# A two-layer GLA and short-convolution step on one core: the sample's state products in column strips, the third token group's LayerNorm moved into the MLP, and the convolution's output projection in plain products

## The chip, the core and the metric

The kernel runs on one core of a Trainium2 chip. Its engines work side by side, each on its own list of instructions: TensorE (PE: matrix products; PEld are its weight loads), VectorE (DVE), ScalarE (ACT), GpSimd (POOL) and SyncE (SP), which here only issues transfers; POOL issues transfers too and sends most of the outputs. The metric is the device time of one execution in microseconds, the median of several runs. A profiled execution gives the trace.

## What is computed

One inference step over 1,056 tokens: a prompt of 1,024 and 8 sequences of 4 new tokens each (the samples). Layer 0 mixes by gated linear attention (GLA), layer 1 by a gated short convolution; a dense squared-ReLU MLP follows each. Cut to what matters:

```
D_MODEL, D_FF, GLA_HEADS = 1024, 4096, 4           # per head 128 q/k and 256 v channels
# GLA:  S_t = diag(exp(g_t)) S_{t-1} + k_t^T v_t ;  o_t = q_t S_t
#       each of the 8 sample sequences starts from a state s0 of its own (128 x 256 per head)
o = o * rsqrt(mean(o*o) + RMS_EPS) * norm_g;  f = (o * silu(r)) @ w_o
# convolution:
bg, cg, h = split(x @ w_in, 3);  u = cg * h
conv = sum_i full[:, i:i+t] * w_conv[i]            # full = the 2 rows of state, then u
f = (bg * conv) @ w_out                            # w_out is 1024 x 1024
# MLP:  f = square(relu(x @ w_up)) @ w_down
# after each of the four:  x = LayerNorm(ALPHA * x + f(x))
```

All is fp32. A product runs as three products of split operands: each operand is a high part (rounded to fp32r) and a low part (the rest), and high times high, high times low and low times high are added in PSUM.

## The kernel before, in words

Channels lie on partitions, tokens along the free axis. ScalarE makes a high part (`A.copy`) and VectorE the low part (`V.tensor_sub`): L847 and L848 in `split`, tiles `wh`/`wl` for weights and `bh`/`bl` for activations.

**GLA** works on three token groups, `TGS`, of 384, 384 and 288 tokens; the third holds the last 256 prompt tokens and the 32 sample tokens. Heads 0 to 3 come in turn. `ACC[tg]` (the tile `Z`) gathers the output projection over the heads. Projections are products of 384 or 288 columns from lines L236 to L238 (`mm3`), 24 of them for each unit of 128 output channels and each group. `mm` (L232) is a product in fp32 itself, and the trace shows each as two instructions. `sample(h)` treats the sample tokens of one head: its inner `outputs` makes 32 columns for each of two 128-channel halves `m`, from a product with the values `vt` plus, for each of the eight sequences, q (4 columns) times its own state `s0`. `outputs` is followed by `products` and `state`, which renew the state.

What runs beside what in this stage is a set of chains. `after(key, (delay, fn), ...)` puts one on, `tick()` runs the steps whose delay, in an estimated clock, has passed, and `need(key)` runs at once what is left of it. A scheduler then orders the instructions of PE, ACT and DVE; SP and POOL keep the written order. At the last head each group's output projection (`accumulate`, from `out(tg)`) ends in `layer_norm(tg, ...)`: the means are taken away, the squares added up, a product with ones (L309) gives the variance, `rstd` follows in ring tiles, and four `finish` steps multiply (L334, VectorE, two channel tiles each) and scale (L336, ScalarE, one channel tile each). All three chains end before the MLP begins.

**MLP and convolution** share a machine. A `Unit` is a weight tile of 128 x 512 (256 KB): loaded plainly (`raw`, on SP's queue) or as a sum of quarters (tile `SB`, the first part on SP's queue, the rest added by accumulating transfers on POOL's). `up` and `down` multiply in a scheme of seven products of matrix quarters in place of eight; sums of activations and outputs that the scheme needs are VectorE's. Tokens are cut in two halves of 528 (`TH`), and `product` (L865) does 3 matmuls for each of two tiles of 264 columns (`NT`). The work is a list of steps (`step`, `hook`), each with `prep` (split its weights and activations), `work_` (the matmuls) and `done`; `prep` runs two steps ahead. PSUM tiles there are four `ps2` of 1,024 columns.

L865 runs 13,440 matmuls: 5,376 in the first MLP, 2,016 in the convolution's input projections, 672 in its output projection (`down(..., True)`, seven products by four pairs) and 5,376 in the second MLP. After each `down` `norm(z, t, ...)` takes the LayerNorm of half `t` over five tiles of tokens: transposes by PE to tokens on partitions (L1175, eight a tile), statistics on VectorE, scaling on ScalarE (L1194), transposes back (L1202, eight a tile), and an eviction that applies gain and bias (L1206 on ScalarE, L1210 on VectorE). `states` writes out the convolution's new states.

Names of PSUM tiles are `ps` (GLA) and `pq` (later); `big` are norm's row tiles.

Of the kernel before, what the change touches and what calls it, by code (L numbers as in the profile page):

```python
# [9 lines left out]
F32 = mybir.dt.float32  # L10
# [3 lines left out]
ALU = mybir.AluOpType  # L14
# [43 lines left out]
def hybrid_step(ctx, tc, x_prompt, x_sample, state_gla, state_conv, gla_w_in, gla_w_gate_up, gla_b_gate,  # L58
# [91 lines left out]
    for g in (2, 3):  # L150
        V.tensor_add(seq, seq, seq1[:, g, :])


# [162 lines left out]
    def layer_norm(tg, sums, pg, pb):  # L316

        n = TGS[tg][1]
        z = ACC[tg]
        box = {}  # L320

        def split():
# [9 lines left out]
        def finish(k):  # L332
            pair = z[:, k:k + 2, :]
            V.tensor_tensor(pair, pair, box["rstd"][:, :n].unsqueeze(1).to_broadcast([P, 2, n]), op=ALU.mult)  # L334
# [126 lines left out]
    with tc.tile_pool(name="gp", bufs=3) as gp:  # L461
# [109 lines left out]

        def gated(tg, m, ur, o, tags=("g", "g")):
            n = TGS[tg][1]
# [7 lines left out]
            V.tensor_mul(sr[:, :n], o[:, m, :n], sr[:, :n])  # L581
            hh = gt(tags[0], [P, 384], 9 if tags[0] == "g" else 3, F32R)
            A.copy(hh[:, :n], sr[:, :n])
            hl = gt(tags[1], [P, 384], 9 if tags[1] == "g" else 3, F32R)
            V.tensor_sub(hl[:, :n], sr[:, :n], f32(hh[:, :n]))
            return hh[:, :n], hl[:, :n]

        def core(h, qkk, uv, dec, o):
# [77 lines left out]
            def sample(k2t, st, vt):  # L666
# [3 lines left out]
                box = []  # L670

                def outputs():
                    po = ps()
# [25 lines left out]

                after(("sample",), (0, outputs))  # L700

# [30 lines left out]
        for h in range(H):  # L732
# [34 lines left out]
            for tg in range(3):  # L767
                tags = [("g", "g")] * 2
                if last and tg == 2:
                    tags = [("b", "g"), ("b", "b")]  # L770
                hs.append([gated(tg, m, ur[m], o[tg], tags[m]) for m in range(2)])
                if tg == 2:
# [17 lines left out]
    explog()  # L790
    for tg in range(3):
        need(("x", tg))
# [19 lines left out]
    SB = work.tile([P, NB, 512], F32, name="SB")  # L812
    cbuf = work.tile([P, KC * 34], F32, name="cbuf")
    cst = cbuf[:, 0:KC * 16].rearrange("p (j s) -> p j s", s=16)
# [53 lines left out]
    class Unit:  # L868
# [33 lines left out]
        def split(self):  # L902
# [3 lines left out]
            return self.parts  # L906

    in_sb = {}
    ONE, TWO, SUM, ON1, ON2 = (11000,), (15000, 9000), (21000, 14000), (12000,), (17000, 9000)
# [5 lines left out]
    EARLY = ("sum", (21, 22), SUM)  # L915
    ALL = ("sum", (11, 12, 21, 22), (40000, 32000, 24000, 16000))

# [10 lines left out]
    def up(x, pairs, relu):  # L928
# [62 lines left out]
        for prod in UP:  # L991
            for i, (s, quad) in enumerate(pairs):
# [26 lines left out]
    def down(z, pairs, last, final=False):  # L1019
# [54 lines left out]
        def down_units(prod, g, *where):  # L1074
            if prod == 3 and n == 4:

                us = [Unit(pairs[i][1], ALL, i, *where) for i in g]
            else:
                us = [Unit(pairs[i][1], WDOWN[prod], pairs[i][0], *where) for i in g]
            return us, [Unit(pairs[i][1], EARLY, pairs[i][0]) for i in g if prod == 1]  # L1080
# [178 lines left out]
    def conv(x, z):  # L1259
# [40 lines left out]

        def quad_out(j):
            def q(ij):
                i, k = ij // 10 - 1, ij % 10 - 1
                r = (j + 4 * k) * P
                return conv_w_out[0, r:r + P, i * 512:i * 512 + 512]
            return q

        for g in range(2):
            js = (2 * g, 2 * g + 1)
# [53 lines left out]
    def rows_out(t):  # L1363
# [11 lines left out]
        if t < 6:  # L1375
            A.mul(yt[:tn, :], yt[:tn, :], r)  # L1376
        return (lambda: nc.gpsimd.dma_start(yt[:tn, :], end[1][:tn, :], accum_op=ALU.add),  # L1377
                lambda: nc.sync.dma_start(out, yt[:tn, :]))

    mlp(0, Z, Z2)  # L1380
    conv(Z2, Z)
# [54 lines left out]
```

## Time and profile before

| | |
|---|---|
| median of 3 runs | 2261.52 us (2258.97 to 2264.5) |
| the profiled execution | 2263.59 us, of which 2261.9 us are the span of the trace and 1.69 us lie around it |
| granted TensorE clock, mean | 0.983 |
| busy | PE 97%, DVE 72%, ACT 50%, POOL 23% |
| transfers | 251.51 MB, mean 111 GB/s |
| stages, by the trace | GLA's last product ends at 513 us; of L865 the first MLP's 5,376 matmuls begin at 531, the 2,016 of the convolution's input at 1202, the 672 of its output at 1455, the second MLP's at 1561; the last ends at 2244 |

The profiled execution is 2.07 us above the median. A count `xN` is a number of instructions. The idle time printed behind a group or in square brackets is that of the engine just before it, and what stands behind the arrow is what ended it. `PEclk` is the TensorE clock that was granted (1.00 is full speed). In rows of windows each engine's busy time is followed by its instructions, then come PEclk, the share of the DMA engines in use and GB/s.

### The profile page before, as it was taken

The numbers are of one execution on the slowest core, as the hardware profiler recorded it, in microseconds if no ns is written. First come the engines' busy times: TensorE is split into PE (matmuls) and PEld (weight loads), VectorE is DVE, ScalarE is ACT, GpSimd is POOL, SyncE is SP. The second block draws the span as 40 slices with busy tenths as digits, with TensorE's granted clock in tenths as the row PEclk, the third lists the DMA queues.
The fourth block names the chain that finished last, engine by engine and source line by source line (L and its number), as shares of the span: only waits on it lengthen the run. The fifth ranks groups of instructions, "written<-read, shape, count | busy, mean of one in ns | idle before, by whom it ended". The sixth has DMA issues, their size and how long they took to land. (4 is left out here: it accounts for less than half of the span.)

```text
span 2261.9 us, 43193 instructions
## 1 busy us (share of the span) xinstructions
PE 2202.5 (97%) x17341; PEld 2180.1 (96%) x17341; DVE 1619.5 (72%) x2982; ACT 1127.8 (50%) x2023; POOL 524.7 (23%) x551
## 2 busy tenths in 40 slices
PE   9999999996999999999999999998999999999996
PEld 8999999996999999999999999997999999999996
DVE  7474848467578864678787897996668875578877
ACT  4443525258563445564457444445855444654443
POOL 5202321221422021412021323220331101422121
PEclk9999999998999999999999999998999999999998
DMA  5120212113868456769353857760786734877546
GB/s 156 32 75 31 75 40 67 38 59 81 109 119 214 119 108 122 97 126 217 99 112 68 131 111 100 164 156 24 126 136 141 177 90 95 129 131 185 152 88 148
DMA packets 297476, 251.51 MB, mean 111 GB/s; under 512 B 15444, under 2 KB 238776, under 8 KB 297276
## 3 DMA queue, kind: packets, MB, share of 16 engines
q0 software_dynamic: 123200, 107.58, 31.2%
q1 hardware_dynamic: 174076, 141.18, 21.1%
q8 instruction: 136, 2.23, 0.4%
q14 instruction: 64, 0.52, 0.1%
HBM read 227.00 MB, written 9.12 MB: 104 GB/s over the span
## 5 line engine op out<-in xcount | busy, mean ns | idle before, releaser
L865 PE MATMUL pq<-bh,wh 128*128 128x264 f32 x4160 | 847.6, 285 | 9.3 <-ACT bh L847 7.3
L865 PE MATMUL pq<-bl,wh 128*128 128x264 f32 x4160 | 847.7, 285 | 5.0 <-DVE bl L848 5.0
L865 PE MATMUL pq<-bh,wl 128*128 128x264 f32 x4160 | 845.0, 285 | 1.8 <-DVE wl L848 1.7
L865 PEld LDWEIGHTS pq<-bh,wh 128*128 128x128 f32 x4160 | 646.2, 189 | 11.5 <-ACT bh L847 9.9
L865 PEld LDWEIGHTS pq<-bl,wh 128*128 128x128 f32 x4160 | 646.3, 189 | 6.1 <-DVE bl L848 5.8
L865 PEld LDWEIGHTS pq<-bh,wl 128*128 128x128 f32 x4160 | 646.2, 189 | 2.6 <-DVE wl L848 2.5
L847 ACT CAST wh<-raw 128x512 fp32r<-128x512 f32 x312 | 193.5, 621 | 398.2 <-PE pq L865 383.7
L848 DVE TENSOR_TENSOR wl<-raw,wh 128x512 fp32r<-128x512 f32 x312 | 214.4, 688 | 142.2 <-ACT wh L847 135.2
L854 POOL DMA_DIRECT2D SB<-in_mlp_w_up x128 | 163.5, 1329 | 430.8 <-DVE wl L848 223.8
L847 ACT CAST wh<-SB 128x512 fp32r<-128x512 f32 x208 | 128.7, 619 | 239.2 <-PE pq L865 213.4
L848 DVE TENSOR_TENSOR wl<-SB,wh 128x512 fp32r<-128x512 f32 x208 | 142.7, 686 | 85.3 <-ACT wh L847 85.3
L847 ACT CAST bh<-H 128x528 fp32r<-128x528 f32 (+1 forms) x292 | 165.3, 570 | 56.7 <-PE pq L865 51.3
L848 DVE TENSOR_TENSOR bl<-H,bh 128x528 fp32r<-128x528 f32 (+1 forms) x292 | 179.0, 625 | 15.4 <-ACT bh L847 15.2
L854 POOL DMA_DIRECT2D SB<-in_mlp_w_down x96 | 85.1, 1172 | 300.3 <-DVE wl L848 136.6
L236 PE MATMUL ps<-XH,whi 128*128 128x384 f32 (+1 forms) x384 | 128.6, 335 | 0.0
L237 PE MATMUL ps<-XL,whi 128*128 128x384 f32 (+1 forms) x384 | 127.5, 332 | 0.0
L238 PE MATMUL ps<-XH,wlo 128*128 128x384 f32 (+1 forms) x384 | 127.0, 331 | 0.0
L854 POOL DMA_DIRECT2D SB<-in_conv_w_in x48 | 61.2, 1295 | 168.8 <-DVE wl L848 60.4
L865 PE MATMUL pq<-bh,rh 128*128 128x264 f32 x320 | 94.0, 294 | 4.0 <-ACT bh L847 4.0
L865 PE MATMUL pq<-bl,rh 128*128 128x264 f32 x320 | 91.9, 287 | 0.2
L865 PE MATMUL pq<-bh,rl 128*128 128x264 f32 x320 | 91.5, 286 | 0.0
L963 ACT ACTIVATE H<-H 128x528 f32<-128x528 f32 x96 | 61.9, 645 | 46.9 <-DVE H L983 28.0
(275 smaller groups left out, 3620.4 us busy)
## 6 DMA issues: line engine op xcount, KB each, us to landing
raw<-in_mlp_w_down SPq DMA_DIRECT2D x160, 256.0 KB, 3.2
SB<-in_mlp_w_up POOLq DMA_DIRECT2D x128, 256.0 KB, 4.9
raw<-in_mlp_w_up SPq DMA_DIRECT2D x96, 256.0 KB, 2.9
SB<-in_mlp_w_down POOLq DMA_DIRECT2D x96, 256.0 KB, 7.8
SB<-in_mlp_w_up SPq DMA_DIRECT2D x64, 256.0 KB, 4.3
raw<-in_gla_w_in SPq DMA_DIRECT2D x24, 512.0 KB, 3.8
SB<-in_conv_w_in POOLq DMA_DIRECT2D x48, 256.0 KB, 4.8
raw<-SB POOLq DMA_DIRECT2D x36, 256.0 KB, 4.2
```

What stands on the lines that cost most here:

```text
L236: PE.matmul(out, wh, xh, start=first, stop=False)
L237: PE.matmul(out, wh, xl, start=False, stop=False)
L238: PE.matmul(out, wl, xh, start=False, stop=last)
L847: A.copy(hi[:, :w], src)
L848: V.tensor_sub(lo[:, :w], src, f32(hi[:, :w]))
L854: queue.dma_start(dst, src, **kw)
L865: PE.matmul(out[:, c:c + NT], w, b[:, n * NT:(n + 1) * NT], start=first and i == 0, stop=last and i == 2)
L963: A.activation(h, h, AF.Relu, scale=sign)
```

## The change

**First part, `sample`.** The 64 products of 4 columns in a head's `outputs` go. In their place `inter` multiplies the q of all 32 sample tokens (a weight of 32 columns) by all eight states, as eight products of 256 columns; each product writes one of four strips of 32 PSUM partitions, so that partition 32g + t holds token t times the state of sequence g or 4 + g. Two VectorE instructions multiply by the masks `seq` (each token keeps its own sequence) and leave `x` in a ring tile; in `outputs`, 2000 units of the chains' clock later, one product for each `m` with `rep4` (four unit matrices, one upon another) adds up the strips. `products` and `state` come later by the same distance. On PE (the first head; what lies between are the next unit's projections):

```order
L232 MATMUL ps_1271<-sTs,vt_1197 128x32
L232 MATMUL ps_1271<-g_605,raw_1025 128x4 x4
L232 MATMUL ps_1271<-g_605,raw_1027 128x4 x4
L232 MATMUL ps_1271<-sTs,vt_1197 128x32
L232 MATMUL ps_1271<-g_605,raw_1025 128x4 x4
L232 MATMUL ps_1271<-g_605,raw_1027 128x4 x4
L236 MATMUL ps_1298<-XH_92,whi_685 128x384
```

and now, with the 24 projection products between the two pieces:

```order
L693 MATMUL ps_1276<-raw_1030,g_610 32x256 x4
L693 MATMUL ps_1276<-raw_1032,g_610 32x256 x4
```

```order
L239 MATMUL ps_1332<-sTs,vt_1202 128x32
L239 MATMUL ps_1332<-rep_136,ring_1285 128x32
L239 MATMUL ps_1332<-sTs,vt_1202 128x32
L239 MATMUL ps_1332<-rep_136,ring_1285 128x32
L500 MATMUL ps_1345<-gl_375,w_gate 128x384
```

Here `raw` is s0, `g` the q, and `rep` the matrix rep4. The small products with the states are gone from `outputs`, and the sum over strips stands one projection behind the products that it sums.

**Second part, the third group's LayerNorm.** At the last head `out(0)` and `out(1)` stand ahead of the third group's `gated` products. The third group's `layer_norm` only adds the two sums of squares into `cbuf`; the variance, `rstd` and the finish are steps of `last_tokens`, whose chain runs in the first MLP's products 1 and 2, which read the first half of the tokens alone, and are at an end by product 5 (`need(("x", 2))`). In the first two groups every other channel tile of `finish` is scaled by VectorE (L351) in place of ScalarE, and the second group's steps fall due earlier. On VectorE, ahead of the first activations split for the MLP, before (`bl` is the first of these):

```order
L297 SCALAR_TENSOR_TENSOR ring_5802<-ring_5805,ring_5802 128x384
L289 TENSOR_SCALAR ring_5829<-ps_5826 128x288
L334 TENSOR_TENSOR Z<-Z,ring_5802 128x2x384 x4
L295 TENSOR_TENSOR ring_5834<-ring_5831 128x288
L848 TENSOR_TENSOR wl_5931<-raw_5928,wh_5930 128x512
L296 SCALAR_TENSOR_TENSOR ring_5834<-ring_5834,ring_5829 128x288
L848 TENSOR_TENSOR wl_5937<-raw_5934,wh_5936 128x512
L297 SCALAR_TENSOR_TENSOR ring_5831<-ring_5834,ring_5831 128x288
L334 TENSOR_TENSOR Z<-Z,ring_5831 128x2x288 x4
L848 TENSOR_TENSOR bl_5913<-Z,bh_5912 128x528
```

and now (L345 is L334 before, L304 is L297, L281 is L274, L870 is L848):

```order
L304 SCALAR_TENSOR_TENSOR ring_5718<-ring_5722,ring_5718 128x384
L273 TENSOR_TENSOR Z<-Z,ps_5806 128x288
L345 TENSOR_TENSOR Z<-Z,ring_5718 128x2x384 x2
L351 TENSOR_SCALAR Z<-Z,par 128x384 x2
L345 TENSOR_TENSOR Z<-Z,ring_5718 128x2x384 x2
L351 TENSOR_SCALAR Z<-Z,par 128x384 x2
L281 TENSOR_TENSOR ring_5793<-ring_5793,ring_5814 128x288
L870 TENSOR_TENSOR wl_5878<-raw_5875,wh_5877 128x512
L330 TENSOR_TENSOR cbuf<-ring_5793,ring_5711 128x288
L870 TENSOR_TENSOR bl_5882<-Z,bh_5881 128x528
```

The 288-column steps of `rstd` and `finish` have left this place; four scalings of 384 columns have come.

**Third part, the convolution's output projection.** `conv_out` takes plain products in place of the seven: first half 0 of the tokens (for each half of the output channels `mg` eight steps `k` of 24 matmuls), then half 1 (for each `mg` two tiles of tokens `n`, each of eight steps of 12). That is 768 matmuls for 672. Its 32 weight tiles (16, each loaded twice) all come plainly on SP's queue; before there were 20 such transfers and 8 into `SB` on SP's, and 24 accumulating ones on POOL's. The first half's norm follows its last product as a hook, and the second half's norm is put on in two parts, after the tiles `n = 0` and `n = 1` of the last `mg`. `places` regroups the tiles that hold the gated inputs, and `back` restores them. On PE, at the end of the projection and its norm, before (`rl` are resident weights' low parts; the last row is the second MLP's):

```order
L865 MATMUL pq_18746<-bh_18733,rl_18621 128x264
L1202 MATMUL pq_18790<-ident,big_18410 128x128 x8
L1175 MATMUL pq_18800<-ident,Z 16x128 x8
L1202 MATMUL pq_18823<-ident,big_18410 128x128 x8
L1202 MATMUL pq_18833<-ident,big_18410 128x16 x8
L1175 MATMUL pq_18879<-ident,Z 128x128 x8
L865 MATMUL pq_18960<-bh_18851,wh_18786 128x264 x2
```

and now (L887 is L865 before, L1254 is L1202, L1227 is L1175):

```order
L887 MATMUL pq_18816<-bh_18937,rh_18749 128x264
L887 MATMUL pq_18816<-bl_18938,rh_18749 128x264
L887 MATMUL pq_18816<-bh_18937,rl_18750 128x264
L1254 MATMUL pq_19015<-ident,big_18183 128x128 x8
L887 MATMUL pq_19051<-bh_18967,wh_18963 128x264 x2
```

Only eight transposes are left between the projection's last product and the MLP's first.

The diff, cut (`SB` is no longer used by the projection; explog() is a table switch of ScalarE):

```diff
@@ setup, const pools
+    cbuf = const.tile([P, 288], F32, name="cbuf")
+    rep4 = gconst.tile([P, NS], F32, name="rep4")
+    V.tensor_add(rep4, ident[:, 0:NS], ident[:, NS:2 * NS])
+    for g in (2, 3):
+        V.tensor_add(rep4, rep4, ident[:, g * NS:(g + 1) * NS])
@@ layer_norm
+        if tg == 2:
+            V.tensor_add(cbuf, sums[0][:, :n], sums[1][:, :n])
+            return
...
             for i in (k, k + 1):
-                A.activation(z[:, i, :], z[:, i, :], AF.Identity, scale=par[:, pg + i:pg + i + 1],
-                             bias=par[:, pb + i:pb + i + 1])
-        after(("x", tg), (1500, split), (D_VAR - 1500, var), (D_RSTD, rstd), *[(D_FIN, lambda k=k: finish(k)) for k in range(0, KC, 2)])
+                if i == k:
+                    A.activation(z[:, i, :], z[:, i, :], AF.Identity, scale=g, bias=b)
+                else:
+                    V.tensor_scalar(z[:, i, :], z[:, i, :], g, b, op0=ALU.mult, op1=ALU.add)
+        d_var, d_rstd, d_fin = (1500, 100, 100) if tg else (D_VAR - 1500, D_RSTD, D_FIN)
+        after(("x", tg), (1500, split), (d_var, var), (d_rstd, rstd), *[(d_fin, lambda k=k: finish(k)) for k in range(0, KC, 2)])
@@ sample
+                def inter():
+                    pi = ps()
+                    for j in range(2):
+                        for g in range(4):
+                            PE.matmul(pi[g * NS:(g + 1) * NS, j * DV:(j + 1) * DV], q_[:, off:off + NS], s0[j][:, g, :],
+                                      start=True, stop=True)
+                    cost(DV, 8)
+                    x = ring()[:, :DV]
+                    V.tensor_scalar(x, pi[:, 0:DV], seq[:, 0:1], None, op0=ALU.mult)
+                    V.scalar_tensor_tensor(x, pi[:, DV:2 * DV], seq[:, 1:2], x, op0=ALU.mult, op1=ALU.add)
+                    box.append(x)
...
                         mm(po[:, m * NS:(m + 1) * NS], vt[:, ms], st, stop=False)
-                        for i in range(NSEQ):
-                            c = i * LSEQ
-                            mm(po[:, m * NS + c:m * NS + c + LSEQ], s0[i // 4][:, i % 4, ms],
-                               q_[:, off + c:off + c + LSEQ], start=False, stop=i == NSEQ - 1)
+                        mm(po[:, m * NS:(m + 1) * NS], x[:, ms], rep4, start=False)
...
-                after(("sample",), (0, outputs))
+                after(("sample",), (0, inter), (2000, outputs))
@@ the last head's tail
                 if last and tg == 2:
-                    tags = [("b", "g"), ("b", "b")]
+                    out(0)
+                    out(1)
...
             if last:
-                explog()
-                out(0)
-                out(1)
-            if last:
                 out(2)
...
-    for tg in range(3):
+    for tg in range(2):
         need(("x", tg))
@@ first MLP
+    def last_tokens():
...
+        after(("x", 2), (3000, split_), (3000, var), (3000, rstd_),
+              *[(3000, lambda k=k: finish(k)) for k in range(0, KC, 2)])
...
                         if prod == 5:
                             need(("ln", 1))
+                            need(("x", 2))
@@ conv
-        hooks[1] = states
-        norms(z, col["ln1g"] + KC, col["ln1b"] + KC)
-        down(z, [(4 + j, quad_out(j)) for j in range(4)], True)
+        conv_out(z)
...
+    def conv_out(z):
...
+        for t in range(2):
+            for mg in range(2):
+                ws = {}
+                for n in range(1 + t):
+                    accs = {}
+                    for k in range(KC):
...
+                            us = [Unit(lambda _, rows=rows: rows, ("raw", (0,), ONE), 0, *(("r", NB, wbox) if t else ()))]
...
+                            b2["b"] = split(h[:, n * NT:(n + 1) * NT] if t else h[:, :], TH, "b", 5)
...
+                        step(prep, work_, finish, 12 if t else 24, us)
+                    if (t, mg) == (0, 0):
+                        hook(states)
+                    elif (t, mg) == (0, 1):
+                        hook(lambda: norm(z, 0, (0, 1, 2, 3, 4), *ln))
+                    elif (t, mg) == (1, 1):
+                        hook(lambda n=n: norm(z, 1, ((0, 1), (2, 3, 4))[n], *ln))
```

More of the change, by code (lines that the diff above doesn't have):

```diff
@@ L335, in finish @@
             for i in (k, k + 1):
-                A.activation(z[:, i, :], z[:, i, :], AF.Identity, scale=par[:, pg + i:pg + i + 1],
-                             bias=par[:, pb + i:pb + i + 1])
-        after(("x", tg), (1500, split), (D_VAR - 1500, var), (D_RSTD, rstd), *[(D_FIN, lambda k=k: finish(k)) for k in range(0, KC, 2)])
+                g, b = par[:, pg + i:pg + i + 1], par[:, pb + i:pb + i + 1]
+                if i == k:
[4 more added lines that the diff above has]
+        after(("x", tg), (1500, split), (d_var, var), (d_rstd, rstd), *[(d_fin, lambda k=k: finish(k)) for k in range(0, KC, 2)])
     waiting = []
@@ L570, in rms, with gated @@
             after(("rms", tg), (300, squares), (1500, split), (1500, var), (500, norm))
-        def gated(tg, m, ur, o, tags=("g", "g")):
+        def gated(tg, m, ur, o):
             n = TGS[tg][1]
@@ L767, in hybrid_step @@
             for tg in range(3):
-                tags = [("g", "g")] * 2
                 if last and tg == 2:
-                    tags = [("b", "g"), ("b", "b")]
-                hs.append([gated(tg, m, ur[m], o[tg], tags[m]) for m in range(2)])
+                    out(0)
+                    out(1)
+                hs.append([gated(tg, m, ur[m], o[tg]) for m in range(2)])
                 if tg == 2:
@@ L812, in hybrid_step @@
     SB = work.tile([P, NB, 512], F32, name="SB")
-    cbuf = work.tile([P, KC * 34], F32, name="cbuf")
     cst = cbuf[:, 0:KC * 16].rearrange("p (j s) -> p j s", s=16)
@@ L906, in split, with split_, var, rstd_ @@
             return self.parts
+    def last_tokens():
+        n, z = TGS[2][1], ACC[2]
+        room = big()
+        v, y, t = (room.rearrange("p a b -> p (a b)")[:, i * n:(i + 1) * n] for i in range(3))
+        box = {}
+        def split_():
+            box["parts"] = split(cbuf, TH, "b", 5)
+        def var():
+            box["var"] = ps2()[:, 0:n]
+            for i, part in enumerate(box["parts"]):
+                PE.matmul(box["var"], ones_r, part[:, 0:n], start=i == 0, stop=i == 1)
+            cost(n, 2)
+        def rstd_():
+            V.tensor_scalar(v, box["var"], LN_EPS, None, op0=ALU.add)
+            A.activation(y, box["var"], AF.Ln, bias=epst[LN_EPS])
+            A.activation(y, y, AF.Exp, scale=-0.5)
+            V.tensor_mul(t, y, y)
+            V.scalar_tensor_tensor(t, t, -0.5, v, op0=ALU.mult, op1=ALU.mult)
+            V.scalar_tensor_tensor(y, t, 1.5, y, op0=ALU.add, op1=ALU.mult)
+        def finish(k):
+            pair = z[:, k:k + 2, :]
+            V.tensor_tensor(pair, pair, y.unsqueeze(1).to_broadcast([P, 2, n]), op=ALU.mult)
+            for i in (k, k + 1):
+                A.activation(z[:, i, :], z[:, i, :], AF.Identity, scale=par[:, col["ln1g"] + i:col["ln1g"] + i + 1],
+                             bias=par[:, col["ln1b"] + i:col["ln1b"] + i + 1])
+        after(("x", 2), (3000, split_), (3000, var), (3000, rstd_),
+              *[(3000, lambda k=k: finish(k)) for k in range(0, KC, 2)])
     in_sb = {}
@@ L915, in hybrid_step @@
     EARLY = ("sum", (21, 22), SUM)
-    ALL = ("sum", (11, 12, 21, 22), (40000, 32000, 24000, 16000))
     steps = []
@@ L1074, in down_units @@
         def down_units(prod, g, *where):
[L1075 to L1079, printed above, removed]
+            us = [Unit(pairs[i][1], WDOWN[prod], pairs[i][0], *where) for i in g]
             return us, [Unit(pairs[i][1], EARLY, pairs[i][0]) for i in g if prod == 1]
@@ L1299, in quad_in, with places @@
             return q
[L1301 to L1306, printed above, removed]
+        def places():
+            a, b, c, d = (HQ[q] for q in (11, 22, 21, 12))
+            own.extend((a, b))
+            for q, u, v, s in ((11, c, a, 0), (12, c, a, 4), (21, d, b, 0), (22, d, b, 4)):
+                HQ[q] = u[s:s + 4] + v[s:s + 4]
+        own = []
+        hook(places)
         for g in range(2):
@@ L1378, in rows_out @@
                 lambda: nc.sync.dma_start(out, yt[:tn, :]))
+    last_tokens()
     mlp(0, Z, Z2)
```

41 lines of the change are left out of this document (39 added, 2 removed).

## The prediction

> **What bounds the kernel now.** I read the page's busy times and slices first, then the waits of PE and the chain of waits, then the three places that the change touches, by windows and timelines.
>
> ```profile
> PE 2202.5 (97%) x17341; PEld 2180.1 (96%) x17341; DVE 1619.5 (72%) x2982; ACT 1127.8 (50%) x2023; POOL 524.7 (23%) x551
> PE   9999999996999999999999999998999999999996
> DVE  7474848467578864678787897996668875578877
> ```
>
> PE is busy 97% of the span. The three places where its row falls to 6 or 8 are the seam from GLA to the MLP (tenth slice), the end of the convolution (28th) and the end of the kernel. So time is won by giving PE less to do or by filling those holes. What PE waited for:
>
> ```profile
> PE pq L865 <- ACT bh L847: 11.3, 4, 6.9
> PE ps L309 <- DVE ring L304: 9.5, 1, 9.5
> PE pq L1202 <- ACT big L1194: 8.7, 3, 3.8
> PE pq L865 <- DVE bl L848: 5.0, 3, 2.4
> ```
>
> The columns are total us, times, longest. The single 9.5 (the third group's variance) and the single 6.9 (the MLP's first activations) are the seam; the waits for `big` and most of the rest are the norm around the convolution's end. The chain gives the price of a product of the split kind:
>
> ```profile
> 1598.05 588.88 PE pq L865 x4836
> ```
>
> 4,836 products in 588.88 us: 0.1218 each, with nothing between.
>
> **First part, the sample products.** The rows hold start, duration and kind; the windows (PE, PEld, DVE, ACT, POOL, then PEclk) take the four heads in turn: first the tiny products, then the stretch at half clock behind them.
>
> ```profile
> 98.52 1.93 PE L232 MATMUL ps<-g,raw 128*128 128x4 f32 x16
> 105.54 0.33 PE L236 MATMUL ps<-XH,whi 128*128 128x384 f32 x1
> ...
> 108.00 0.34 PE L238 MATMUL ps<-XH,wlo 128*128 128x384 f32 x1
> 108.26 1.15 PE L232 MATMUL ps<-vt,ring 32*128 32x256 f32 x16
> 330.16 0.39 PE L232 MATMUL ps<-sT,vt 128*128 128x128 f32 x2
> 330.38 0.39 PE L232 MATMUL ps<-qx,S 128*128 128x128 f32 x2
> ```
>
> ```profile
> 98.38:102.62 4.24, 4.24 (x37) 4.24 (x37) 1.27 (x3) 2.70 (x4) 0.00 (x0) 0.93 0.00 0
> 102.62:105.41 2.79, 2.79 (x10) 2.79 (x11) 1.46 (x2) 2.59 (x4) 0.00 (x0) 0.50 0.00 0
> 218.00:222.37 4.37, 4.37 (x38) 4.37 (x37) 1.27 (x3) 2.70 (x4) 0.00 (x0) 0.90 0.00 0
> 222.37:228.29 5.92, 5.92 (x20) 5.92 (x21) 2.40 (x3) 5.67 (x9) 0.00 (x0) 0.50 0.26 69
> 339.59:343.52 3.93, 3.93 (x37) 3.93 (x37) 1.27 (x3) 2.70 (x4) 0.00 (x0) 1.00 0.03 6
> 344.34:347.75 3.41, 3.41 (x12) 3.41 (x11) 1.84 (x2) 3.35 (x5) 0.00 (x0) 0.50 0.00 0
> 461.42:466.77 5.35, 5.35 (x38) 5.35 (x37) 1.27 (x3) 2.70 (x4) 0.00 (x0) 0.72 0.00 0
> 466.77:470.63 3.86, 3.86 (x13) 3.86 (x14) 1.84 (x2) 3.63 (x6) 0.00 (x0) 0.50 0.00 0
> ```
>
> A product of 4 columns costs 1.93/16 = 0.12, nearly a product of 264 columns, and behind 32 of them the granted clock stands at 0.50. The four runs of tiny products take 4.24 + 4.37 + 3.93 + 5.35 = 17.89. The stretches behind them take 15.98 for 10 + 20 + 12 + 13 = 55 projection products; at full clock fourteen of them lie from 105.54 to 108.00, 0.176 each, so 15.98 − 55 × 0.176 = 6.3 are lost. Before: 24.2.
>
> Now there are sixteen instructions of 256 columns a head. The nearest row is the state's products at 108.26, also 16 of 256 columns and four deep, in strips of rows: 1.15. In a line, 128 columns cost 0.22/2 = 0.11 (330.16 to 330.38), so sixteen of 256 would cost 16 × 0.22 = 3.5. I take 1.15, because both kinds put four independent strips into the array; what speaks against it is that a column strip reads all rows. Eight small instructions stay in `outputs` (two `vt`, two `rep4`, doubled): 8 × 0.12 = 1.0. After: 4 × 2.1 = 8.4, and no half clock, since neither piece is long by itself. **Gain 15.8.** The bounds: strips in a line, 4 × 4.5 = 18.0, gain 6.2 (0, if the clock then falls as before); and 18 if the small ones cost half.
>
> [...] No column strips are in the trace before. [...]
>
> VectorE's two instructions have 24 projection products (24 × 0.176 = 4.2) to run beside; I cost them and rep4's three additions at nothing. Were that cover gone, two masks of 256 columns would cost less than 1 us a head. `state` is late by one projection; the next reader of its tiles is the next head's load, far off.
>
> **Second part, the seam.** I count from where the third group's output products begin, 506.40.
>
> ```profile
> 506.40 0.29 PE L236 MATMUL ps<-b,whi 128*128 128x288 f32 x1
> 522.76 0.61 PE L309 MATMUL ps<-ring,ones_r 128*128 128x288 f32 x1 [9.52 <-DVE ring L304]
> 531.13 1.69 PE L865 MATMUL pq<-bh,wh 128*128 128x264 f32 x6 [6.93 <-ACT bh L847]
> 524.62 3.55 DVE L334 TENSOR_TENSOR Z<-Z,ring 128x768 f32<-128x768 f32 x4
> 519.16 1.03 DVE L274 TENSOR_TENSOR ring<-ring,ring 128x288 f32<-128x288 f32 x1 [0.34 <-ACT ring L269]
> 533.96:538.90 4.94, 4.94 (x22) 4.94 (x23) 4.94 (x9) 4.94 (x9) 0.00 (x0) 0.50 0.01 3
> ```
>
> ```profile
> L266 DVE TENSOR_TENSOR Z<-Z,ps 128x288 f32<-128x288 f32 x24 | 10.5, 450 | 3.8 <-PE ps L238 3.8
> L1210 DVE TENSOR_SCALAR Z<-Z,par 128x528 f32<-128x528 f32 x32 | 15.6, 559 | 2.4 <-ACT Z L1206 2.3
> L848 DVE TENSOR_TENSOR wl<-raw,wh 128x512 fp32r<-128x512 f32 x312 | 214.4, 688 | 142.2 <-ACT wh L847 135.2 <-PE pq L1175 3.1 <-PE pq L865 2.2
> L848 DVE TENSOR_TENSOR bl<-H,bh 128x264 fp32r<-128x264 f32 x80 | 32.9, 424 | 15.3 <-ACT bh L847 15.2
> ```
>
> From 506.40 to steady products at 533.96 are 27.6; the third group's two projections (48 products of 288 columns at 0.176 × 288/384 = 0.13, 6.3) lay ahead of it and now lie behind `out(1)`, so that 33.9 are to be compared. After: 48 projection and 48 output products 12.6, two variance products of the second group 0.35, and the last accumulation (L266, 0.45) on VectorE about 0.8 behind: 13.8. What must follow on VectorE before the MLP's first activations: the second group's multiplication 3.55, four scalings of 384 columns at 0.559 × 384/528 = 0.41 (1.6), the last sum of squares 1.03, a weight's low part 0.69, the `cbuf` sum 0.45 and `bl` 0.70 = 8.0. That gives 21.8, and the third group's variance products, now in the MLP, 0.3: **gain 11.8.** VectorE is the wait that is left; ScalarE's half of the scalings runs beside it. The half clock behind the seam (22 products in 4.94 for 2.7) I leave as it is; without it 2.3 more are won. The bounds: 5, if all of VectorE's second-group work waits for the last accumulation with its rstd steps too; and 17, if multiplication and scaling are done under PE's 12.6. `last_tokens` finishes in the MLP's products 1 and 2, some 190 us of cover (two sevenths of the 5,376 products, at 0.1218); I cost its steps on VectorE at nothing, because there VectorE's digits are 5 to 8. Were it not done by product 5, its four multiplications, less than 3.55, would stand bare.
>
> **Third part, the output projection.**
>
> ```profile
> 0.00:1455.44 1455.44, 908.56 (x7393) 903.10 (x7393) 0.98 0.48 102
> 1455.44:1601.03 145.59, 130.58 (x1035) 127.17 (x1034) 114.42 (x242) 76.95 (x141) 19.67 (x23) 0.95 0.45 106
> 1470.10:1520.04 49.94, 48.35 (x393) 47.65 (x393) 49.38 (x82) 24.08 (x45) 13.73 (x18) 1.00 0.78 177
> 1542.70:1560.62 17.92, 12.85 (x108) 11.72 (x105) 9.91 (x31) 8.89 (x15) 0.00 (x0) 0.97 0.00 1
> 1560.62:1579.19 18.57, 12.40 (x64) 11.79 (x65) 10.74 (x28) 6.86 (x14) 0.00 (x0) 0.66 0.05 14
> 1542.07 0.87 PE pq L1175 x8
> ```
>
> The first row counts L865 alone: 7,392 are done at 1455.44, so the output projection begins there. From there to 1601.03, where the chain's unbroken stretch has begun, PE runs 672 + 192 products = 864 × 0.1218 = 105.2, and nine tiles of transposes, there and back, 9 × 2 × 0.87 = 15.7, with 0.3 for the states. The other 24.4 are waits and half clock: VectorE is full between 1470 and 1520 (49.38 of 49.94), and the norm stands bare in the two windows behind 1542.70, where PE is busy 25.2 of 36.5.
>
> Now 96 products more, 96 × 0.1218 = **11.7 lost**. The stretch is 768 + 192 = 960 products, 116.9, transposes and states 16.0, and what stays bare. The first half's norm has the second half's 384 products (46.8) to run beside. Part of the second half's norm follows the last product, beside the MLP's first, which read the first half alone. VectorE has per step of the first half 0.69 + 0.71 (528 columns for 512) of 24 × 0.1218 = 2.9, in the second half 0.69 + 0.42 = 1.1 of 1.46 where weights are split. So I leave 1 each for the last taps, a change of halves and the states: 3.0. After 135.9, **gain 9.7**. The bounds: nothing bare, 12.7; and 0, if 12.7 stay bare.
>
> Where it would fail is the load:
>
> ```profile
> raw<-in_conv_w_out SPq DMA_DIRECT2D x20, 256.0 KB, 4.6
> 1490.00:1496.00 6.00, 6.00 (x51) 6.00 (x50) 6.00 (x11) 2.48 (x5) 3.56 (x4) 1.00 0.97 291
> ```
>
> All 32 tiles of 256 KB, 8.4 MB, go through SP's queue. A tile per 2.9 us is 90 GB/s, one per 1.46 is 179. The trace held 177 over fifty us and 291 over six, by both queues; a tile took 4.6 from issue to landing, and six may be on their way. I cost it at nothing. POOL loses 24 issues, for which nothing waited.
>
> **The sum.** 15.8 + 11.8 + 9.7 = 37.3; the profiled execution's own time, 2263.59, less 37.3 is 2226.3. It is 2.07 above the median of the runs, 2261.52, so against that it would be 2224; I say **2225**.
>
> **Rivals.**
> B, the strips run in a line: 18.0 instead of 8.4, gain 27.7, **2235**. For it: every product uses all rows. Against: outputs and weights are apart. 0.15.
> C, the convolution wins nothing: the second half's norm and splits overfill VectorE (1.1 of 1.46 before the norm adds its own), and 12.7 stay bare. Gain 27.6, **2235**. 0.15.
> D, the seam gives 5: VectorE's row is long and rstd may come late. Gain 30.5, **2232**. 0.08.
> E, the other side: SP's queue alone doesn't feed the second half. The other parts give 27.6; slower begins where the projection's stretch takes 145.6 + 27.6 = 173.2 instead of 135.9, so 37.3 of waiting; the 768 products and these waits are 93.5 + 37.3 = 130.8, and 8.4 MB in that time is 64 GB/s. The trace held 177 and more. At 60 GB/s, 140 us, **2272**. 0.04.
> F, no change: the gains go into new waits at the same places, as a norm that is late in the MLP's first step. **2263**. 0.03.
> My forecast has 0.55.
>
> **Range and chances.** The forecast's own range is 2215 (seam 17, half clock gone, convolution 12.7: 48.1) to 2232 (seam 8, convolution 7). With B, C and D it reaches to 2243 (2243.8 against the median with B and C together); below, all upper bounds give 2263.6 − 18 − 19.3 − 12.7 = 2213.6, and 1 less against the median. I take 2212 to 2243. By more than 0.2% (4.5 us, about what a measurement of this kernel tells from no change) faster: forecast, B, C, D 0.93; the same 0.03; slower, E, 0.04.
>
> **What would show it.** In the changed trace: the strips' row, 16 of 256 columns, 1.15 (right) or 3.5 (B); no half clock behind it in GLA; the first L887 product about 22 behind the third group's first projection product; L887's output projection, first to last, near 98, with 250 GB/s nowhere needed; waits of PE on `wl` or `wh` there would be E, waits for `big` or `bl` C. The whole is wrong if PE waits at a place that I called covered: for `rep4`'s ring, for SP's weights, or for `last_tokens` at product 5.

## The result and the profile after

The changed kernel took 2226.39 us (median; 2225.98 to 2228.03), the kernel before beside it 2260.55. The ratio is 0.9848 with a 95% interval of 0.9831 to 0.9865: 1.5% faster, 2225 forecast. The profiled execution took 2226.24 with a span of 2224.5, 37.4 less than before. The page's first rows:

```profile
PE 2187.1 (98%) x17389; PEld 2163.1 (97%) x17389; DVE 1604.6 (72%) x2968; ACT 1119.7 (50%) x2025; POOL 504.3 (23%) x527
PE   9999999989999999999999999999999999999996
PEclk9999999999999999999999999999999999999998
```

PE has 48 instructions more and 15 us less busy time; the hole at the convolution's end (the 28th slice) is gone, the one at the seam is an 8 for a 6. PE's waits, four largest (total us, times, longest), where the 9.5 for the variance and the waits for `big` have left:

```profile
PE pq L887 <- ACT bh L869: 10.6, 2, 7.2
PE pq L887 <- DVE bl L870: 2.8, 1, 2.8
PE pq L887 <- DVE wl L870: 1.7, 2, 0.9
PE ps L316 <- DVE raw L723: 1.6, 1, 1.6
```

**The first part's rows.** The first head's pieces on PE (its tiny products took 4.24 before), each with the product that starts next:

```profile
95.16 1.07 PE L693 MATMUL ps<-raw,g 128*32 128x256 f32 x16
96.16 0.44 PE L243 MATMUL ps<-XH,whi 128*128 128x384 f32 x1
100.45 0.30 PE L239 MATMUL ps<-sTs,vt 128*128 128x32 f32 x2
100.59 0.39 PE L239 MATMUL ps<-rep,ring 128*128 128x32 f32 x2
101.26 0.42 PE L500 MATMUL ps<-gl,w_gate 96*128 96x384 f32 x1
```

The sixteen take 1.0 until the next product starts, the eight small ones 0.8 (100.45 to 101.26). Behind none of the four heads is there a stretch at half clock.

**The seam.** PE's rows that answer to those before, with the window from the first low part's product to the end of the half clock; then VectorE's list while PE waits:

```profile
487.98 1.20 PE L243 MATMUL ps<-g,whi 128*128 128x288 f32 x7 [0.38 <-ACT g L599]
501.83 1.69 PE L887 MATMUL pq<-bh,wh 128*128 128x264 f32 x6 [7.16 <-ACT bh L869]
506.31 0.81 PE L887 MATMUL pq<-bl,wh 128*128 128x264 f32 x2 [2.78 <-DVE bl L870]
506.31:511.33 5.02, 5.02 (x23) 5.02 (x24) 3.37 (x6) 0.22 (x1) 0.00 (x0) 0.50 0.44 126
```

```profile
494.88 0.56 DVE L302 TENSOR_TENSOR ring<-ring 128x384 f32<-128x384 f32 x1
495.36 0.45 DVE L273 TENSOR_TENSOR Z<-Z,ps 128x288 f32<-128x288 f32 x1
495.72 0.79 DVE L303 SCALAR_TENSOR_TENSOR ring<-ring,ring 128x384 f32<-128x384 f32 x1
496.43 0.44 DVE L273 TENSOR_TENSOR Z<-Z,ps 128x288 f32<-128x288 f32 x1
496.80 0.78 DVE L304 SCALAR_TENSOR_TENSOR ring<-ring,ring 128x384 f32<-128x384 f32 x1
497.50 0.44 DVE L273 TENSOR_TENSOR Z<-Z,ps 128x288 f32<-128x288 f32 x1
497.87 2.65 DVE L345 TENSOR_TENSOR Z<-Z,ring 128x768 f32<-128x768 f32 x2
500.44 1.34 DVE L351 TENSOR_SCALAR Z<-Z,par 128x384 f32<-128x384 f32 x2
501.70 1.81 DVE L345 TENSOR_TENSOR Z<-Z,ring 128x768 f32<-128x768 f32 x2
503.43 0.86 DVE L351 TENSOR_SCALAR Z<-Z,par 128x384 f32<-128x384 f32 x2
504.21 0.45 DVE L281 TENSOR_TENSOR ring<-ring,ring 128x288 f32<-128x288 f32 x1
504.58 0.68 DVE L870 TENSOR_TENSOR wl<-raw,wh 128x512 fp32r<-128x512 f32 x1
505.18 0.45 DVE L330 TENSOR_TENSOR cbuf<-ring,ring 128x288 f32<-128x288 f32 x1
505.55 1.32 DVE L870 TENSOR_TENSOR bl<-Z,bh 128x528 fp32r<-128x528 f32 x2
```

PE's last output product ends at 494.67. VectorE is busy 11.56 of the 11.64 us from there to 506.31, where the end of the first `bl` lets PE go on. The steps of the second group's `rstd` (L302 to L304) stand between the last accumulations (L273), so that the last of these ends at 497.94; by the starts, the three steps take 1.9 us of it.

**The output projection.** From its first product to the second MLP's 193rd, window and load:

```profile
1428.08:1563.90 135.82, 135.61 (x1130) 134.39 (x1129) 93.66 (x212) 79.34 (x151) 6.01 (x7) 1.00 0.32 90
raw<-in_conv_w_out SPq DMA_DIRECT2D x32, 256.0 KB, 3.0
```

PE is busy 135.61 of 135.82 at full clock. VectorE does 93.66 for 114.42 before, and the 32 tiles on one queue land sooner (3.0 us) than the 20 did (4.6).

**By stages.** In all kernels below the same six marks can be found on PE: *a*, the variance product ahead of the first sample products; *T*, the third group's first output product; the first MLP's product 200, counted from 0 (*200th* in the table and below); the output projection's first; the second MLP's 193rd; the end. Each stage in us, from one profiled execution each (differences of starts):

| | to a | a to T | T to 200th | to the projection | projection | rest |
|---|---|---|---|---|---|---|
| before | 98.0 | 408.4 | 53.5 | 895.6 | 145.6 | 660.9 |
| after | 94.7 | 393.3 | 44.5 | 895.6 | 135.8 | 660.6 |
| after, again | 95.1 | 393.3 | 44.7 | 895.6 | 135.9 | 661.3 |
| first part alone | 96.5 | 391.8 | 53.0 | 895.6 | 147.4 | 660.9 |
| second part alone | 95.9 | 407.4 | 43.6 | 895.6 | 146.7 | 661.7 |
| third part alone | 96.7 | 406.7 | 54.0 | 895.6 | 135.7 | 660.6 |
| without the second | 97.2 | 391.7 | 53.2 | 895.6 | 135.7 | 660.5 |

Each part changes its own stage and no other by more than about 2 us, and the work between is the same to 0.1. The first column isn't the change's: it runs from 94.7 to 98.0 with a stretch at half clock near 10 us, whose length differs between executions (0, 3.4 and 6.8 us in these traces; two traces of the changed kernel have none, and the one with the strips in another order, below, has 3.4). The profiled execution before had the longest:

```profile
9.83:16.66 6.83, 6.59 (x22) 5.97 (x23) 4.57 (x4) 2.12 (x3) 3.92 (x3) 0.50 0.95 338
```

So about 3 of the 37.4 us between the two traces are chance, and the medians differ by 34.2. One execution of the second part alone, at a granted clock of 0.746, took 2675.63 us and is left out of the medians below.

### The profile page after: what moved, and what is told of

Same layout as the page of the kernel before. It is cut to its first block, busy times and chain, and to the rows that moved or that the text cites. A ratio compares the mean times of both kernels' runs of the same rounds, so it can differ in the third digit from the quotient of the medians.

```text
span 2224.5 us, 43242 instructions
## 1 busy us (share of the span) xinstructions
PE 2187.1 (98%) x17389; PEld 2163.1 (97%) x17389; DVE 1604.6 (72%) x2968; ACT 1119.7 (50%) x2025; POOL 504.3 (23%) x527
## 4 chain that ended last, share of the span: by engine, by line
PE 92%; DVE 5%; ACT 1%; DMA 1%; issue 0%; POOL 0%; DVEq 0%; ACTq 0%; POOLq 0%
PE pq L887 72%; PE ps L243 5%; PE ps L245 5%; PE ps L244 5%; PE ps L239 2%; PE pq L1227 1%; DMA SB<-in_mlp_w_down 1%; PE pq L1254 1%; DVE H L1328 0%; DVE Z L345 0%; DVE bl L870 0%; DVE stats L1210 0%; DVE Z L1483 0%; DVE Z L273 0%; DVE wl L870 0%
## 5 line engine op out<-in xcount | busy, mean ns | idle before, releaser
L887 PE MATMUL pq<-bh,wh 128*128 128x264 f32 x4128 | 839.9, 285 | 7.2 <-ACT bh L869 7.2
L887 PE MATMUL pq<-bl,wh 128*128 128x264 f32 x4128 | 839.7, 284 | 2.8 <-DVE bl L870 2.8
L887 PE MATMUL pq<-bh,wl 128*128 128x264 f32 x4128 | 837.5, 285 | 1.7 <-DVE wl L870 1.7
L887 PEld LDWEIGHTS pq<-bh,wh 128*128 128x128 f32 x4128 | 640.2, 189 | 8.2 <-ACT bh L869 7.4
L887 PEld LDWEIGHTS pq<-bl,wh 128*128 128x128 f32 x4128 | 640.4, 189 | 3.6 <-DVE bl L870 3.4
L887 PEld LDWEIGHTS pq<-bh,wl 128*128 128x128 f32 x4128 | 640.2, 189 | 2.2 <-DVE wl L870 2.1
L870 DVE TENSOR_TENSOR wl<-raw,wh 128x512 fp32r<-128x512 f32 x308 | 211.9, 688 | 145.3 <-ACT wh L869 138.7
L870 DVE TENSOR_TENSOR wl<-SB,wh 128x512 fp32r<-128x512 f32 x208 | 142.8, 687 | 85.7 <-ACT wh L869 85.6
L870 DVE TENSOR_TENSOR bl<-H,bh 128x528 fp32r<-128x528 f32 (+1 forms) x304 | 183.3, 615 | 25.7 <-ACT bh L869 25.5
L887 PE MATMUL pq<-bh,rh 128*128 128x264 f32 x384 | 112.8, 294 | 3.7 <-ACT bh L869 3.5
L887 PE MATMUL pq<-bl,rh 128*128 128x264 f32 x384 | 110.2, 287 | 0.2
L887 PE MATMUL pq<-bh,rl 128*128 128x264 f32 x384 | 109.6, 285 | 0.0
L243 PE MATMUL ps<-whi,XH 128*128 128x256 f32 (+1 forms) x288 | 84.5, 293 | 0.0
```

The source lines that it names most:

```text
L243: PE.matmul(out, wh, xh, start=first, stop=False)
L870: V.tensor_sub(lo[:, :w], src, f32(hi[:, :w]))
L887: PE.matmul(out[:, c:c + NT], w, b[:, n * NT:(n + 1) * NT], start=first and i == 0, stop=last and i == 2)
```

## The experiments

**Each part alone.** The kernel before with the diff's hunks of one part: `inter`, rep4 and the chain in `sample`; `layer_norm`, the tail, `last_tokens` and `cbuf`; `conv_out`, `places` and `back`.

> The kernel before with the first part alone (inter in place of the tiny products). Theory: in the trace after, the head start is 3.1 us ahead of the first sample product (98.03 before, 94.89 after) and grows to 19.4 us at the third group's last gated products, so this part is worth 19.4 - 3.1 = 16.3 us: about 2244 us against 2260.5, one row of 16 products of 1.1 us a head, and no half clock behind it. The 3.1 us are a stretch of half clock at the kernel's start (9.83 to 16.66 us) that need not be the part's doing. Rival: the 3.1 us belong to it too; 19.4 us, about 2241 us, and each execution of the kernel before loses them. Second rival: part of the gain is only shifted and comes back as waits at the seam; under 12 us, above 2248 us.

2246.08 us against 2259.79, ratio 0.9939 (0.9926 to 0.9951). The stage is 391.8, 15 to 16.6 less than in the three traces without this part. By medians the gain is 13.7 (11.1 to 16.7), so the first rival's 19.4 falls. The second rival's 12 lies within the interval, but the waits at the seam that it needs are not there (53.0 for 53.5).

> The kernel before with the second part alone (third group's LayerNorm in the MLP). Theory by the two traces: from the third group's gated products to steady MLP products 33.9 us before and 25.6 after, so 8.3 us: about 2252 us, with VectorE the wait at the seam (rstd's four steps among the last accumulations, then 8.4 us of finish, sums and splits). Rival, the prediction's term of 11.8 us: about 2249 us, if the 3.5 us that are missing were lost to the other two parts. Second rival: nothing, about 2260 us, if last_tokens costs elsewhere what the seam wins.

2254.19 us, ratio 0.9976 (0.9966 to 0.9985): 5.4 us, less than the theory's 8.3, and its interval (3.4 to 7.7) holds neither that nor 11.8. The seam's stage itself is as short as in the changed kernel (43.6). What the window left out is shown by the run without the second part, below.

> The kernel before with the third part alone (output projection in plain products). Theory: 145.6 us before and 135.8 after from the first output product to the second MLP's 193rd product, so 9.8 us: about 2251 us; PE's waits there go from about 24 to about 3 us while 96 products cost 11.7. Rival: the gain needs the other parts (the clock's phase, the place of cbuf); under 5 us, above 2255 us.

2250.86 us, ratio 0.9959 (0.9946 to 0.9971), stage 135.7: the third part needs no other. The three parts alone give 13.7 + 5.6 + 8.9 = 28.2 by medians, the whole 34.2; each median is uncertain by 2 to 3 us, so I read sums from the stages. Part of the difference may be half clock: in the traces of the first and of the second part alone there are 17.07 us of it around the end of the projection, in the kernel before 13.65, and that stage is 1.8 and 1.1 us longer; with the third part there is none.

**The strips.** First the order of the sixteen, then all in one strip:

```diff
-                    for j in range(2):
-                        for g in range(4):
+                    for g in range(4):
+                        for j in range(2):
                             PE.matmul(pi[g * NS:(g + 1) * NS, j * DV:(j + 1) * DV], ...
```

> The changed kernel with inter's two loops exchanged: strip 0 for both halves of the sequences, then strip 1, and so on; the same sixteen products, but neighbours mostly in the same strip. Theory: products run side by side only when neighbours lie in different strips; the row of 16 goes from 1.07 us to between 2.5 and 3.5 us (in line 16 x 0.22), 6 to 10 us in all, about 2233 to 2236 us. Rival: the order doesn't matter (short weights or another cause make them cheap): 1.07 us and 2226 us.

2228.23 us (ratio 0.986, 0.9846 to 0.9873), a to T 393.3 as in the changed kernel, and the row:

```profile
97.75 1.09 PE L693 MATMUL ps<-raw,g 128*32 128x256 f32 x16
```

The theory as I had put it is wrong: neighbours need not lie in different strips. Four instructions start together every 0.2 us in both orders. They start 7 ns apart where two instructions in a row belong to one strip, and 13 where four do.

For one strip, the masks and the sum over strips are cut to its 32 partitions too, and three of every four sequences are missing from the outputs (the diff, cut):

```diff
-PE.matmul(pi[g * NS:(g + 1) * NS, j * DV:(j + 1) * DV], ...
+PE.matmul(pi[0:NS, j * DV:(j + 1) * DV], ...
```

> The changed kernel with all sixteen instructions of a head writing strip 0 (the masks and the sum then read one strip; the other three sequences of each half are left out of the outputs). Theory (products of different strips run side by side, whatever their order within the sixteen): in one strip they run in line, 16 x 0.22 = 3.5 us instead of 1.07, so 4 x 2.4 = 9.7 us more, about 2236 us. Rival: a weight of 32 columns is cheap by itself, 1.07 us and 2226 us.

2236.91 us, ratio 0.9899 (0.9884 to 0.9914). The rows, with neighbours:

```profile
95.23 3.64 PE L693 MATMUL ps<-raw,g 128*32 128x256 f32 x16
98.80 0.44 PE L243 MATMUL ps<-XH,whi 128*128 128x384 f32 x1
```

3.64 instead of 1.07, one instruction every 0.216; a to T is 403.9 for 393.3. Side by side, the strips are worth 10.6 us in four heads. The theory holds.

**The late norm.** The hook of the first half's norm goes behind the tile `n = 0` of the second half's last `mg`:

```diff
-                    elif (t, mg) == (0, 1):
-                        hook(lambda: norm(z, 0, (0, 1, 2, 3, 4), *ln))
                     elif (t, mg) == (1, 1):
+                        if n == 0:
+                            hook(lambda: norm(z, 0, (0, 1, 2, 3, 4), *ln))
```

> The changed kernel, but the first half's norm is put on only behind the last tile but one of the output projection, as late as the seven products forced it. The products, weights and splits stay. Theory (the gain of the third part is that this norm now lies beside the second half's 384 products): 10 to 20 us stand bare again, the stretch from the first output product to the second MLP's 193rd takes 146 to 156 instead of 135.8, half clock at its end; 2237 to 2247 us. Rival (the gain comes from less VectorE work: no sums and no accumulations of the seven products): under 3 us, below 2230 us.

2239.86 us, ratio 0.9907 (0.989 to 0.9925), the stage 147.6. PE's waits in it:

```profile
PE pq L1254 <- ACT big L1246: 7.4, 3, 3.2
PE pq L887 <- ACT bh L869: 1.6, 1, 1.6
```

There are 9.0 us of waits, and 6.83 us of half clock from 1544.03 on. The place of this norm alone, with 384 products to run beside or with 96, is worth 11.8 us (147.6 for 135.8), no less than the stage gained in all (9.8 to 11.7). With the norm late, plain products take what seven took (145.6 to 147.4). What pays for the 96 products more, VectorE's lighter list or the rest of the order, was not tried by itself.

**Without the second part.** The kernel before with the first and third.

> The changed kernel without its second part (the kernel before with the first and the third). By the windows the second part is worth 9 us (third group's output to the 200th MLP product 53.5 before, 44.5 after), by the medians of its run alone 5.4 of 2260. Theory: the windows hold here too, 44.5 becomes 53, so 2235 to 2236 us. Rival: part of the 9 us is taken back elsewhere, 2231 to 2233 us.

2233.92 us, ratio 0.9882 (0.9867 to 0.9898): the second part is worth 6.6 to 7.5 us beside the two medians of the changed kernel (2226.39; 2227.27 when run again). The time lies between the theory's range and the rival's. T to the 200th is 53.2, as the theory says, but a to T is 1.6 shorter than with the second part: there the rival is right, and the rows say where most of the 1.6 goes. The changed kernel, ahead of T (the first group's two variance products, then the second group's first):

```profile
478.59 0.34 PE L316 MATMUL ps<-ring,ones_r 128*128 128x384 f32 x1
479.36 0.45 PE L317 MATMUL ps<-ring,ones_r 128*128 128x384 f32 x1 [0.43 <-DVE ring L312]
487.09 0.34 PE L316 MATMUL ps<-ring,ones_r 128*128 128x384 f32 x1
```

The second group's variance products (0.35) lie ahead of T now, before behind it, and there are two small waits (0.43, and 0.38 in T's own row above): 1.2 of the 1.6. So the seam's gain is 8.5 to 9 less 1.6: about 7 to 7.5.

**The seam made shorter.** What bounds it is VectorE's list. A first variant, x1, leaves of the second group's channels 4 to 7 only the multiplication at the seam. Their scaling, which nothing reads before the MLP's second product, goes behind it, and channels 0 to 3 are scaled by ScalarE (the diff, cut):

```diff
-                if i == k:
+                if tg and k >= 4:
+                    rest.append((i, z[:, i, :], g, b))
+                elif i == k or tg:
                     A.activation(z[:, i, :], z[:, i, :], AF.Identity, scale=g, bias=b)
...
+    after(("rest",), *[(2500, lambda a=a: scaled(*a)) for a in rest])
     last_tokens()
```

> The changed kernel with less VectorE work at the seam: of the second group's finish, channels 0 to 3 are scaled by ScalarE alone, and the scaling of channels 4 to 7 (4 x 0.47 us on VectorE, 4 x 0.71 on ScalarE) comes in the MLP's first product, which does not read them. Theory (VectorE's list is the wait of the seam): the first product with a low part starts 1.9 us earlier, 16.4 instead of 18.3 us behind the third group's first output product; 2224.5 us, more (up to 2.5) if the half clock is avoided too. Rival: ScalarE (four scalings of 0.71 and the splits of the weights) takes VectorE's place: first product no earlier than 18, no change, 2226.4.

2225.54 us, ratio 0.9846 (0.9832 to 0.9861). PE's rows of the MLP's first products:

```profile
502.60 1.25 PE L890 MATMUL pq<-bh,wh 128*128 128x264 f32 x4 [7.84 <-ACT bh L872]
504.97 0.81 PE L890 MATMUL pq<-bl,wh 128*128 128x264 f32 x2 [1.12 <-DVE bl L873]
```

The first product with a low part comes 16.9 behind T (488.08 here), 1.4 sooner (1.9 expected). The first with high parts alone now comes later, 14.5 for 13.9, behind ScalarE's scalings. The stage is 43.5; half clock comes all the same (from 496.67 for 13.65 us).

A second variant, x2, is x1 with products of unit matrices in the hole, behind `need(("x", 1))`:

```diff
+    warm = ps()
+    for _ in range(24):
+        PE.matmul(warm[:, :P], ident, ident, start=True, stop=True)
     glac.close()
```

> x1_seam_later, and 24 products of unit matrices (48 instructions, about 0.11 us each at full clock, 5.3 us) behind the last output product, where TensorE has nothing to do for 7 us. Theory: the half clock behind the seam (13.7 us of it in the changed kernel, of which 5 to 6 us are busy) comes from the idle time; with products in the hole it doesn't come, or later and shorter, and 2.5 us are won beyond x1: about 2222 us. Rival: the half clock comes anyway (the products are too few or of the wrong kind), same as x1; or they delay the first product and cost 1 to 2 us.

2225.97 us, ratio 0.9849 (0.9834 to 0.9864), stage 43.4. This is not the 2222 that I expected but the rival's "same as x1": the half clock is shorter (6.83 us for 13.65), but of it 5.6 us lie behind the first product with a low part, where x1 has 5.4. The rows:

```profile
494.64 5.52 PE L821 MATMUL ps<-ident 128*128 128x128 f32 x48
502.65 1.00 PE L893 MATMUL pq<-bh,wh 128*128 128x264 f32 x6 [2.48 <-ACT bh L875]
505.02 0.81 PE L893 MATMUL pq<-bl,wh 128*128 128x264 f32 x2 [1.38 <-DVE bl L876]
```

There are two idle pieces, 2.48 and 1.38, and the half clock comes at 503.83, in the second. With 36 products in place of 24 (x3) the first is filled:

> x2_seam_warm with 36 products in place of 24 (72 instructions, 8.2 us), so that TensorE has work until its first product of the MLP is ready at 502.6. In x2 the half clock still came, at 503.8, after 3.86 us of idle time in two pieces. Theory: with one idle piece of 1.4 us left the half clock doesn't come at all; third group's output to the 200th MLP product 41 instead of 43.4, about 2223.5 us. Rival: it comes still, because the wait for the first low part is enough, or the added products delay the first real one: 2225.5 us or more.

2223.83 us, ratio 0.9837 (0.9821 to 0.9853). The windows from T to the first low product, and on to the 200th:

```profile
488.01:504.92 16.91, 15.40 (x126) 15.19 (x126) 16.82 (x30) 14.94 (x29) 5.62 (x5) 1.00 0.35 94
504.92:529.02 24.10, 24.10 (x198) 24.10 (x199) 17.50 (x30) 17.10 (x34) 2.62 (x2) 1.00 0.60 149
```

No half clock comes, and the stage takes 41.0 instead of 43.4 (41 expected). The other executions, which have no trace, fit this: their mean granted clock is 0.996 to 0.997, in x2 0.994 to 0.996. This is the fastest version of all, 2.6 to 3.4 us under the changed kernel's medians; the intervals of the ratios overlap, and it is the stage (44.5 to 41.0) that shows the gain.

## Why the prediction was right

The sum of 37.3 against 37.4 in the traces is closer than its terms, and that is luck: one term was too large, and chance in the profiled execution before made up for it.

1. *First part, 15.8*: the stage gives 15 to 16.6. Strips 1.0 for 1.15, small products 0.8 for 1.0, the half clock gone. That the strips run side by side, which I took from the row strips' row, is shown by the one-strip run (2236.91; rival B forecast 2235). The sixteen take 3.64/1.07 = 3.4 times as long in one strip as in four. In the changed trace all sixteen use every row, four start within some 20 ns (95.16 to 95.18), and four more weight loads start while those run (95.19 to 95.21).
2. *Seam, 11.8*: about 7 to 7.5; this term was mis-sized. The step that failed is "the last accumulation on VectorE about 0.8 behind". It ended 3.3 behind PE (497.94 against 494.67): 2.5 us more, of which `rstd`'s three steps, which stood between the accumulations, are 1.9. I had named that as the lower bound's case. PE's own part took 14.0 for 12.95 (480.70 to 494.67), 0.4 of it a wait. VectorE's list behind took 8.4 for 8.0: its finish cost 6.66 for 3.55 + 1.6 (L345 1.3 each in its first pair, for 0.89), its last sum of squares 0.45 for 1.03. So steady products began 25.6 behind the third group's first gated product (480.70), not 22. Ahead of that place lies a wait of 0.43 that I had not seen, and one group's variance products that lay behind it before. VectorE as the wait that is left was right, and x1 shows it.
3. *Third part, 9.7*: 9.8 to 11.7. Two errors of mine cancel in the 135.9: beside the 960 products PE is busy 18.7 us (135.61 less 116.9), not 16.0, mostly because there are ten tiles to turn, not nine (the fifth of each half has 16 tokens), and the states take 1.0, not 0.3; and of the 3.0 that I left bare only 0.2 are. The norm beside the second half's products was the reason, as the run with the late norm shows. C fell, since no wait for `big` or `bl` is left there, and E too, since none for a weight is: PE's waits in the whole stage are 0.2.
4. What made the sum fit the trace is the start's half clock, about 3 us of chance in the profiled execution before, which makes up for most of the seam. Against the medians the gain was 34.2, and the parts by stages, 16 + 7 + 10 to 11, give 33 to 34.

## What to carry to other kernels

Small products with few weight columns can share the array in column strips (sixteen instructions of 256 columns took 1.07 us in four strips, 3.64 in one), and within sixteen instructions the order of the strips didn't matter (1.09). Avoid long rows of tiny products: behind the 32 of 4 columns the clock stood at 0.50 in every head of the three traces that have them. Put the sum over strips where other products cover VectorE's step. Look for the order of work that puts a norm beside products before counting products: with 96 products more the stage was still 9.8 to 11.7 us shorter. Where a stage boundary leaves PE idle, count what one engine still has in its list, take away what the first product doesn't read, and fill the rest: with idle pieces of 2.48 and 1.38 us the half clock came, with 1.51 in all it didn't.

## What the runs showed of the hardware

- Strips of 32 columns over all 128 rows: sixteen instructions of 256 columns took 1.07 us in four strips, 3.64 in one; one strip's four in a row don't hold up the others (1.09).
- In the changed kernel PE's hole at the seam is 7.16 us and, behind 1.69 of products, 2.78 more: the clock fell to half 3.0 us into it, for 13.65. With 2.48 and 1.38 it fell in the second piece, for 6.83; with 1.51 in all it didn't. These are single traces of three kernels. Eleven stretches of half clock end within the traces of the kernel before and of the changed one: five of 3.41 us, three of 6.83, and one each of 10.24, 13.65 and 20.48, all 3.41 or a multiple. The stretch near 10 us changes from one execution to another (0, 3.4 and 6.8 us); what sets it was not shown.
- VectorE's multiplication of 768 columns took 1.3 us in one pair and 0.9 in the next (2.65 and 1.81 for two). The first pair runs beside POOL's additions of squares (busy for 5.6 us from 495.26), the second behind them. In all thirteen traces every such multiplication at the seam without an addition of POOL's beside it took 0.94 to 0.96; of those beside one, the ones with the second part took 1.18 to 1.55, those without it 1.11 and 0.95. So the slow ones all stand beside POOL, and this is most of what the finish cost too much; that POOL's work is the cause was not tried by moving it.
